# One GpSimd power in place of eleven VectorE operations for every inverse square root of a hybrid decoder layer

## The chip, the cores and the metric

The kernel runs on one core of a Trainium2 chip. The metric is the device time of one execution in microseconds (us). An engine's name in the profile is PE (TensorE, matrix products; PEld is its weight load), DVE (VectorE), ACT (ScalarE), POOL (GpSimd) and SP (SyncE, which here issues the DMAs). Each engine runs its own list of instructions in the order written down at build time; engines wait for each other only through semaphores.

## The reference, cut to what matters

One layer on x of shape (4096, 1024), float32:

```python
h    = rmsnorm(x, g_pre) * (1 + scale) + shift            # norm 1: one value per token
proj = h @ w_in                                            # one input projection, split among three mixers
attn = sliding_window_attention(...) * silu(ag)            # 8 query heads, window 128
y    = rwkv7(...)                                          # 4 heads of 64, delta-rule state
y    = (y - mean) * rsqrt(var + 64e-5) * ln_w + ln_b       # norm 2: one value per token and head
o    = gated_linear_attention(...)                         # 4 heads of 64
o    = o * rsqrt(mean(o * o) + 1e-5) * norm_w              # norm 3: one value per token and head
z    = concat(attn, rwkv, gla) @ w_out
out  = x + gate * rmsnorm(z, g_post)                       # norm 4: one value per token
```

The four `rsqrt` are what the change touches. (The keys of the RWKV mixer are normalised too, but through ScalarE's Ln and Exp, and stay as they are.)

## The kernel before, in words

The 4096 tokens are cut into 16 tiles of 256 (`NS` = 16, `NT` = 256). The program has two big parts.

In the first part (0 to about 1080 us) every tile passes through stages that are Python generators: `stage_a` (norm 1 of x, transposes, `hT`), `stage_p` (the input projections for the two linear mixers), `stage_d` (decays and gates), `stage_qa`, `stage_qb`, `stage_qc` (the RWKV chunk matrices and a triangular inverse, with two trips through DRAM), `stage_q2` (the RWKV state recurrence and norm 2), `stage_r` (gated linear attention and, in `gla_norm`, norm 3), `stage_v`, `stage_k`. Beside them `stage_c` splits the weights of the second part into two float16 halves and `stage_g` computes the adaLN gate on GpSimd. Tiles overlap: while one is in its recurrence, others are in their projections.

In the second part (about 1080 us to the end) each tile has `stage_s` (attention), `stage_m` (the gated mix, scaled and split into float16 halves) and `stage_p2` (gates, q, k, v of the next tiles and the output projection, `outp`). `outp` ends each half tile of 128 tokens with `norm` (norm 4, one column), and in the last tile with `last_norm`, whose result scales the last rows that are written out. For the first half in the last tile (`h` = 1) ScalarE scales and GpSimd adds x in two halves of 512 columns; for the other (`h` = 0) VectorE does both in one operation per half.

`rsqrt(y, v, n)` works on n columns of 128 partitions: n = 2 in `stage_a` (`msx` to `rsx`), 8 in `gla_norm` (`og` to `orr`) and in `stage_q2` (`ve` to `yr`), 1 in `norm` (`sy` to `ry`). It starts from the bit trick with the constant tile `magic` (a shift into tile `nwi`, a subtraction) and makes three Newton steps of three operations each through tile `nwt`: eleven VectorE instructions. `last_norm` has the same in nine (tiles `ln0` to `ln2`, `ln` in the profile), where the ninth also multiplies by `oi`. In all 78 calls of `rsqrt` (16 with n = 2, 32 with n = 8, 30 with n = 1) and two of `last_norm` are executed. A fallback for extreme gates, which calls the same helpers in a loop, is in the program but is not entered with these inputs.

The order on each engine is fixed by a planner, `Order`. `note` books every instruction with a cost (`occ`, how long it holds its engine; `lat`, until others may use the result); `pin`, called once for each part, simulates the five engines as a list scheduler: whichever engine is free takes, of its ready instructions, the one that comes first in the program (shifted by a lag for some stages), and the order that results is pinned. So a changed cost or a changed engine of one instruction changes the order of others too. GpSimd's costs before:

```python
        elif e == "Pool":
            if name == "memset":
                st.occ = 0.06
            elif name == "tensor_copy":
                st.occ = 0.25 if n <= 2 else 0.11 + 0.95e-3 * n
            else:
                st.occ = 0.42 + 1.5e-3 * n if n <= 512 else 1.85e-3 * n
            st.lat = st.occ + 0.05
```

GpSimd's other work in the first part: `tensor_tensor` for `ATm` (`stage_qb`, 32 partitions), `qb` (`stage_r`) and the gate (`gaw`, `gacc`), copies for `tf`, `TT`, `zs`, `zl`, `bl` (the last column of the tile before). In the second part it copies `kT` once a tile and adds x in `last_norm`.

Nearly all instructions are recorded through one helper, so they have line L334 in the profile; the tiles' names tell them apart.

Of the kernel before, what the change touches and what calls it, by code (L numbers as in the profile page):

```python
# [12 lines left out]
F32 = mybir.dt.float32  # L13
BF16 = mybir.dt.bfloat16
I32 = mybir.dt.int32
AF = mybir.ActivationFunctionType
ALU = mybir.AluOpType
# [4 lines left out]
P = 128  # L22
# [41 lines left out]
class Order:  # L64
# [34 lines left out]
    def note(self, eng, name, outs, ins, func, r):  # L99

        st = Step()
        st.ins, st.eng, st.table, st.array, st.bytes, st.then = r.ins, str(eng.engine).split(".")[-1], None, None, 0, []
        st.joint = self.joint
        st.half, st.rank = None, len(self.steps) + self.lag
        e, o = st.eng, outs[0]
        on_psum = [a for a in ins if str(a.tensor.space) == "PSUM"]
        n = max(math.prod(a.shape[1:]) for a in [o, *ins[:1]])
        cols = len([a for a in ins[1:] if math.prod(a.shape[1:]) == 1]) if n > 1 else 0
        if e == "PE":
            f32, lhs = ins[0].dtype == F32, self.region(ins[0])  # L110
            n = math.prod(o.shape[1:])
            _, p0, p1, _ = self.region(o)
            rows, cs = (lhs[1] // 32, (lhs[2] + 31) // 32), (p0 // 32, (p1 + 31) // 32)
            rows, cs = [(0, 4) if b - a > 2 else (a, b) for a, b in (rows, cs)]
            mode = (rows[1] - rows[0], cs[1] - cs[0])
            took = n * (2 if f32 else 1) / 2400 + 0.003
            took = max(took, 0.056 if not f32 else 0.0 if mode[1] < 4 else 0.109 if n > 16 else 0.21)
            issue = 0.017 if f32 and mode == (1, 2) else 0.009 if f32 and mode[0] == 1 else 0.007
            cells = [4 * a + b for a in range(*rows) for b in range(*cs)]
            st.array = (mode, cells, 2 if f32 and name == "matmul" else 1, took, issue)  # L120
            st.occ = st.lat = 0.0
        elif e == "SP":
            st.bytes = math.prod(ins[0].shape) * SIZE[ins[0].dtype]
            kb = st.bytes / 1024
            st.occ = 0.47
            st.lat = next((t for k, t in ((8, 1.9), (32, 2.0), (128, 2.3), (256, 2.6), (512, 3.5)) if kb <= k), 4.8)
        elif e == "Activation":
            st.occ = (0.05 if on_psum else 0.093) + 0.093 * (len(ins) - 1) + 0.832e-3 * n
            st.lat = st.occ + 0.1
            if len(outs) > 1:  # L130
                st.occ += 0.187
                st.lat = st.occ + 0.02
            st.table = LN_TABLE if func == AF.Ln else EXP_TABLE if func in (AF.Exp, AF.Tanh) else None
        elif e == "Pool":
            if name == "memset":
                st.occ = 0.06
            elif name == "tensor_copy":
                st.occ = 0.25 if n <= 2 else 0.11 + 0.95e-3 * n
            else:
                st.occ = 0.42 + 1.5e-3 * n if n <= 512 else 1.85e-3 * n  # L140
            st.lat = st.occ + 0.05
        else:
            if name == "tensor_reduce":
                n = math.prod(ins[0].shape[1:])
            fast = name in ("tensor_scalar", "tensor_single_scalar") and not on_psum and o.dtype == F32
            fixed, rate = 0.065 + 0.06 * (cols > 0), 1.04e-3
            if fast:
                rate = 0.53e-3
            elif name == "transpose":
                fixed = 0.09  # L150
            elif name == "memset":
                fixed, rate = 0.05, 0.3e-3
            elif name == "tensor_tensor" and len(o.shape) == 3 and o.shape[2] <= 16 and n > 16:
                fixed, rate = 0.09, 1.55e-3
            st.occ = fixed + rate * n
            st.lat = st.occ + 0.085

        k, st.needs, st.turn = len(self.steps), {}, []
        out_r, in_r = [self.region(a) for a in outs], [self.region(a) for a in ins]
        if e in ("Activation", "DVE"):  # L160

            st.half = (out_r[0][1], in_r[0][1] if e == "Activation" and in_r and out_r[0][2] - out_r[0][1] <= 64 else None)
        tiles = {a.tensor.name: a.tensor for a in [*outs, *ins]}

        if e == "SP" and self.behind is not None:
            st.turn.append(self.behind)

        def need(j, data=False):
            st.needs[j] = st.needs.get(j, False) or data

        for t, tensor in tiles.items():
            if t not in self.known:
                self.known.add(t)
                if t in self.held and tensor.tag:
                    held = self.slots.setdefault((tensor.owner_uid, tensor.tag), [])

                    if held and self.users.get(held[-1]):
                        st.turn.append(self.users[held[-1]][0])
                    if len(held) == self.held[t]:
                        for j in self.users.get(held.pop(0), ()):  # L180
                            need(j)
                    held.append(t)
            elif t in self.held and self.users.get(t):
                st.turn.append(self.users[t][0])
            if str(tensor.space) == "PSUM":
                for j in self.users.get(t, ()):
                    need(j)

        def meet(a, b):
            return a[1] < b[2] and b[1] < a[2] and (a[3] is None or a[3] & b[3])  # L190

        def covered(a, b):
            return b[1] <= a[1] and a[2] <= b[2] and (a[3] is None or not a[3] & ~b[3])

        for a in in_r:
            for w, j in self.wrote.get(a[0], ()):
                if meet(a, w):
                    need(j, True)
        for a in out_r:
            if a[3] is not None:  # L200
                for old in (self.wrote, self.read):
                    for w, j in old.get(a[0], ()):
                        if meet(a, w):
                            need(j)
                    old[a[0]] = [(w, j) for w, j in old.get(a[0], ()) if not covered(w, a)]
            self.wrote.setdefault(a[0], []).append((a, k))
        for a in in_r:
            self.read.setdefault(a[0], []).append((a, k))
        for t in tiles:
            self.users.setdefault(t, []).append(k)  # L210
        st.needs.pop(k, None)
        self.steps.append(st)
# [186 lines left out]
def hybrid_kernel(ctx, tc, x, rows, ada1, adaw, w1, wl, w2, wo, cst, abias, out):  # L399
    nc = tc.nc  # L400
    model = Model(tc)
    V = Lane(model, nc.vector, *LANES[0])
    S = Lane(model, nc.scalar, *LANES[1])
    G = Lane(model, nc.gpsimd, *LANES[2])
# [7 lines left out]
    cp = pool_of(ctx, "const", 1)  # L412
    dp = pool_of(ctx, "dram", 1, space=DRAM)
    st = pool_of(ctx, "small", 3)
# [7 lines left out]
        a, b = VC[name]  # L422
        return vt[:, a:b] if j is None else vt[:, a + j : a + j + 1]

    magic = cp.tile([P, 16], I32, name="magic")
    V.memset(magic, 0x5F3759DF)

    def rsqrt(y, v, n):
        ii = st.tile([P, 16], I32, tag="nwi", name="nwi")
        tt = st.tile([P, 16], F32, tag="nwt", name="nwt")  # L430
        V.tensor_single_scalar(ii[:, :n], v.bitcast(I32), 1, op=ALU.logical_shift_right)
        V.tensor_tensor(y.bitcast(I32), magic[:, :n], ii[:, :n], op=ALU.subtract)
        for _ in range(3):
            V.tensor_mul(tt[:, :n], y, y)
            V.scalar_tensor_tensor(tt[:, :n], tt[:, :n], -0.5, v, op0=ALU.mult, op1=ALU.mult)
            V.scalar_tensor_tensor(y, tt[:, :n], 1.5, y, op0=ALU.add, op1=ALU.mult)

    def pow2(sc, inv, ss):
        e = st.tile([P, 1], I32, tag="p2e", name="p2e")
# [1437 lines left out]

    def last_norm(f, h, sums, xt):

        v, y, t = [st.tile([P, 1], F32, tag=f"ln{n}", name=f"ln{n}") for n in range(3)]  # L1880
        V.scalar_tensor_tensor(v, sums[:, 0:1], 1e-6, sums[:, 1:2], op0=ALU.add, op1=ALU.add)
        V.tensor_single_scalar(t.bitcast(I32), v.bitcast(I32), 1, op=ALU.logical_shift_right)
        V.tensor_tensor(y.bitcast(I32), magic[:, 0:1], t.bitcast(I32), op=ALU.subtract)
        for c in (3.0, 12.0, 768.0):
            V.scalar_tensor_tensor(t, y, y, v, op0=ALU.mult, op1=ALU.mult)
            V.scalar_tensor_tensor(y, t, -c, y, op0=ALU.add, op1=ALU.mult)
        V.scalar_tensor_tensor(y, y, -1.0 / 8192, f["oi"], op0=ALU.mult, op1=ALU.mult)
        z, r0 = f["end"][h], (NS - 1) * NT + h * P
        for cols in (slice(0, 512), slice(512, 1024)):
            if h:  # L1890
# [176 lines left out]
    with tc.If(flag == 0):  # L2067
# [42 lines left out]
        with tc.For_i(0, NS, 1) as iv:  # L2110
# [9 lines left out]
            for j in range(2):  # L2120
                for n in (2 * j, 2 * j + 1):
                    z = fmx[j][:, 2 * (n % 2) : 2 * (n % 2) + 2, :].rearrange("p b n -> p (b n)")
                    V.scalar_tensor_tensor(z, z, g_h[n], F[0]["ag"][:, 2 * n : 2 * n + 2, :].rearrange("p b n -> p (b n)"),
                                           op0=ALU.mult, op1=ALU.mult)
                S.activation(fbk[:, 0, 0:4], fmx[j], AF.Square, accum_out=fss[:, j : j + 1])
            fsc, foi = mix_scale(fss)
            for j in range(2):
                S.activation(fbk[:, 0, 4 * j : 4 * j + 4], fmx[j], AF.Identity, scale=fsc)
                V.scalar_tensor_tensor(fbk[:, 1, 4 * j : 4 * j + 4], fmx[j], fsc, fbk[:, 0, 4 * j : 4 * j + 4],
                                       op0=ALU.mult, op1=ALU.subtract)  # L2130
# [110 lines left out]
```

## Time and profile before

| what | value |
|---|---|
| device time, median of 3 runs | 2062.37 us (2061.8 to 2066.6) |
| span of the profiled execution, first to last instruction | 2056.7 us; its device time is not listed apart |
| PE busy | 1950.2 us, 95% |
| DVE busy | 1590.3 us, 77% |
| ACT busy | 1130.8 us, 55% |
| POOL busy | 220.5 us, 11% |
| mean granted TensorE clock | 0.986 |

Busy time is a share of the span in which an engine executed something. An engine that is not the bound may idle at no cost. "Idle before, releaser" names what ended an engine's wait. Pipelined matmuls overlap, so a busy PE is not a PE at its peak.

### The profile page before, as it was taken

To read this page: it belongs to the slowest core of one execution; us is meant where nothing else is said; L and a number is where in the kernel's file an instruction comes from. 1 tells how busy PE (TensorE), PEld (TensorE's weight loads), DVE (VectorE), ACT (ScalarE), POOL (GpSimd) and SP (SyncE) were. 2 spreads that over 40 slices of the span, in tenths; PEclk is the share of its full clock that TensorE was granted. 3 is DMA by queue.
4 is the path that set the end of the run, shared out by engine and by line. 5 is a ranking of instruction groups with operands and counts; after the bars stand their busy time and mean duration, and the time that the engine had idled before them with its cause. 6 is when DMAs were issued, how large, how long until landed. Compare 5 with 4: busy or idle time off the path is not lost.

```text
span 2056.7 us, 61151 instructions
## 1 busy us (share of the span) xinstructions
PE 1950.2 (95%) x25123; PEld 1517.8 (74%) x25123; DVE 1590.3 (77%) x5120; ACT 1130.8 (55%) x2609; POOL 220.5 (11%) x405
## 2 busy tenths in 40 slices
PE   6899999999999999999898999999999999999997
PEld 3778787778787778887677677777787777777783
DVE  5877877787778986777667887887777877778877
ACT  5867666667767765664334544444444443444543
POOL 1511112321111121111100000000000000000000
PEclk9999999999999999999999999999999999999999
DMA  9433331433413332113433433433334343334314
GB/s 377 139 106 106 106 94 39 145 124 100 142 61 109 124 93 70 60 53 102 134 109 126 153 112 129 127 127 113 110 115 145 115 130 104 119 121 142 111 46 175
DMA packets 151714, 242.06 MB, mean 118 GB/s; under 512 B 48514, under 2 KB 100226, under 8 KB 147204
## 3 DMA queue, kind: packets, MB, share of 16 engines
q1 hardware_dynamic: 151284, 237.56, 35.6%
q8 instruction: 199, 3.26, 0.7%
q14 instruction: 87, 0.71, 0.1%
q10 hardware_dynamic: 144, 0.52, 0.1%
HBM read 177.20 MB, written 60.82 MB: 116 GB/s over the span
## 4 chain that ended last, share of the span: by engine, by line
PE 62%; DVE 21%; ACT 6%; DMA 6%; issue 3%; SPq 2%; DVEq 0%; POOL 0%; ACTq 0%; POOLq 0%
PE gp L334 16%; PE op L334 12%; PE zz L334 6%; PE qp L334 3%; PE lp L334 3%; PE pv L334 3%; PE kp L334 2%; PE gqk L334 2%; PE sc L334 2%; DVE mtp L334 2%; DVE q L334 2%; PE ovp L334 2%; DVE pr L334 2%; SPq L334 2%; DMA xt<-in_x 1%
## 5 line engine op out<-in xcount | busy, mean ns | idle before, releaser
L334 PEld LDWEIGHTS <-mtp 128*128 128x128 f16 x1344 | 130.4, 98 | 141.8 <-issue 4.6
L334 PE MATMUL op<-o,mtp 128*128 128x512 f16 x768 | 172.3, 379 | 0.1
L334 ACT ACTIVATE pr<-pr,nm,lsc 128x256 f32<-128x256 f32 (+1 forms) x256 | 149.2, 585 | 30.9 <-DVE nm L334 30.8
L334 PE MATMUL op<-ov,mtp 128*128 128x512 f16 x576 | 143.1, 379 | 1.3 <-DMA ov<-woscr 0.8
L334 PEld LDWEIGHTS <-hT 128*128 128x128 f16 x1536 | 118.9, 100 | 26.7 <-DVE kg L334 5.3
L334 DVE CUSTOM_DVE_ANT_0 pr<-sc,ab,kept 128x256 f32<-128x256 f32 (+1 forms) x256 | 108.5, 476 | 10.9 <-PE sc L334 10.2
L334 PE MATMUL pv<-gvh,hT 128*128 128x272 f16 x512 | 102.2, 291 | 6.4 <-DVE kg L334 4.5
L334 DVE TENSOR_TENSOR yv<-op,yv 128x512 f32<-128x512 f32 x105 | 70.4, 682 | 47.8 <-PE op L334 33.6
L334 ACT ACTIVATE ag<-gp,gh 128x512 f32<-128x512 f32 x64 | 43.7, 682 | 111.7 <-PE gp L334 111.7
L334 POOL COPY kT<-kT 128x512 f16<-128x512 f16 x15 | 10.2, 682 | 862.0 <-DVE kT L334 862.0
L334 PE MATMUL gqk<-hT,gqkh 128*128 128x256 f16 x512 | 90.3, 276 | 6.0 <-issue 4.2
L334 ACT ACTIVATE mtp<-yv,oi 128x1024 f16<-128x1024 f32 x30 | 34.3, 1144 | 111.8 <-DVE yv L334 111.3
L334 PE MATMUL qp<-hT,q1h 128*128 128x256 f16 x512 | 87.7, 276 | 5.9 <-DVE kT L334 5.9
L334 PE MATMUL lp<-hT,Lh 128*128 128x256 f16 x512 | 92.9, 276 | 0.2 <-ACT vg L334 0.2
L334 PE MATMUL zz<-hT,kh 128*128 128x256 f16 x512 | 92.3, 274 | 0.0
L334 PE MATMUL zz<-hT,vh 128*128 128x256 f16 x512 | 89.1, 275 | 3.4 <-DVE zb L334 3.4
L334 DVE SCALAR_TENSOR_TENSOR ag<-ag,gp 128x512 f32<-128x512 f32 x64 | 43.8, 684 | 62.4 <-ACT ag L334 62.3
L334 PE MATMUL zz<-hT,rh 128*128 128x256 f16 x512 | 91.8, 279 | 0.0
L334 PE MATMUL gp<-hT,q5h 128*128 128x256 f16 x512 | 87.6, 273 | 0.0
L334 PE MATMUL gp<-hT,q3h 128*128 128x256 f16 x512 | 85.5, 273 | 2.0 <-DVE yv L334 1.4
L334 PE MATMUL qp<-hT,q0h 128*128 128x256 f16 x512 | 85.2, 273 | 0.0
L334 PE MATMUL gp<-hT,q4h 128*128 128x256 f16 x512 | 84.9, 273 | 0.0
(460 smaller groups left out, 5981.7 us busy)
## 6 DMA issues: line engine op xcount, KB each, us to landing
ov<-woscr SPq DMA_DIRECT2D x96, 512.0 KB, 4.4
xt<-in_x SPq DMA_DIRECT2D x16, 1024.0 KB, 5.4
hscr<-hT SPq DMA_DIRECT2D x16, 1024.0 KB, 5.0
hT<-hscr SPq DMA_DIRECT2D x16, 1024.0 KB, 4.8
x<-in_x SPq DMA_DIRECT2D x30, 512.0 KB, 4.2
out<-yv SPq DMA_DIRECT2D x30, 512.0 KB, 2.9
cs<-in_w SPq DMA_DIRECT2D x56, 256.0 KB, 3.5
v<-vscr SPq DMA_DIRECT2D x128, 64.0 KB, 3.7
```

Of the source, the lines that this page charges most:

```text
L334: r = f(*args, **kw)
```

## The change

Each call of `rsqrt` becomes one GpSimd `tensor_tensor` with the operation `pow` and the exponent −0.5 from a constant tile. `last_norm` calls it too, and its ninth operation becomes a plain product with `oi`. The planner gets a cost for small GpSimd operations of at most 8 columns.

```diff
@@ Order.note, GpSimd's costs
             elif name == "tensor_copy":
                 st.occ = 0.25 if n <= 2 else 0.11 + 0.95e-3 * n
+            elif n <= 8:
+                st.occ = 0.33 + 0.165 * n
             else:
                 st.occ = 0.42 + 1.5e-3 * n if n <= 512 else 1.85e-3 * n
@@ hybrid_kernel
-    magic = cp.tile([P, 16], I32, name="magic")
-    V.memset(magic, 0x5F3759DF)
+    expo = cp.tile([P, 8], F32, name="expo")
+    V.memset(expo, -0.5)
 
     def rsqrt(y, v, n):
-        ii = st.tile([P, 16], I32, tag="nwi", name="nwi")
-        tt = st.tile([P, 16], F32, tag="nwt", name="nwt")
-        V.tensor_single_scalar(ii[:, :n], v.bitcast(I32), 1, op=ALU.logical_shift_right)
-        V.tensor_tensor(y.bitcast(I32), magic[:, :n], ii[:, :n], op=ALU.subtract)
-        for _ in range(3):
-            V.tensor_mul(tt[:, :n], y, y)
-            V.scalar_tensor_tensor(tt[:, :n], tt[:, :n], -0.5, v, op0=ALU.mult, op1=ALU.mult)
-            V.scalar_tensor_tensor(y, tt[:, :n], 1.5, y, op0=ALU.add, op1=ALU.mult)
+
+        G.tensor_tensor(y, v, expo[:, :n], op=ALU.pow)
@@ last_norm
-        v, y, t = [st.tile([P, 1], F32, tag=f"ln{n}", name=f"ln{n}") for n in range(3)]
+        v, y = [st.tile([P, 1], F32, tag=f"ln{n}", name=f"ln{n}") for n in range(2)]
         V.scalar_tensor_tensor(v, sums[:, 0:1], 1e-6, sums[:, 1:2], op0=ALU.add, op1=ALU.add)
-        V.tensor_single_scalar(t.bitcast(I32), v.bitcast(I32), 1, op=ALU.logical_shift_right)
-        V.tensor_tensor(y.bitcast(I32), magic[:, 0:1], t.bitcast(I32), op=ALU.subtract)
-        for c in (3.0, 12.0, 768.0):
-            V.scalar_tensor_tensor(t, y, y, v, op0=ALU.mult, op1=ALU.mult)
-            V.scalar_tensor_tensor(y, t, -c, y, op0=ALU.add, op1=ALU.mult)
-        V.scalar_tensor_tensor(y, y, -1.0 / 8192, f["oi"], op0=ALU.mult, op1=ALU.mult)
+        rsqrt(y, v, 1)
+        V.tensor_mul(y, y, f["oi"])
```

## The prediction

> **What bounds the kernel now.** I read the page first (shares, chain), then the span by stretches, then PE's waits, then the timeline of the tail.
>
> ```profile
> span 2056.7 us, 61151 instructions
> PE 1950.2 (95%) x25123; PEld 1517.8 (74%) x25123; DVE 1590.3 (77%) x5120; ACT 1130.8 (55%) x2609; POOL 220.5 (11%) x405
> ...
> PE 62%; DVE 21%; ACT 6%; DMA 6%; issue 3%; SPq 2%; DVEq 0%; POOL 0%; ACTq 0%; POOLq 0%
> ```
>
> PE is the bound and VectorE the second: a fifth of the chain that ended last runs through it. The busy times by stretch (length, then PE, PEld, DVE, ACT, POOL, each with its count) show where that matters.
>
> ```profile
> 120.00:600.00 480.00, 462.19 (x7365) 377.06 (x7364) 373.26 (x1359) 329.94 (x731) 96.31 (x183) 0.99 0.32 100
> 600.00:720.00 120.00, 112.15 (x1728) 90.77 (x1728) 107.99 (x376) 86.63 (x178) 19.74 (x38) 0.97 0.39 124
> 720.00:1080.00 360.00, 340.62 (x5571) 276.69 (x5570) 263.23 (x1010) 192.16 (x431) 53.70 (x105) 0.99 0.28 89
> ...
> 1202.00:1920.00 718.00, 707.43 (x7370) 541.59 (x7369) 560.89 (x1545) 319.28 (x804) 7.36 (x12) 1.00 0.37 120
> ```
>
> From 1202 to 1920 PE is busy 707.4 of 718 us (98.5%). From 120 to 1080 it is busy 462.19 + 112.15 + 340.62 = 915.0 of 960 us, so 45.0 us idle; VectorE is busy 373.26 + 107.99 + 263.23 = 744.5 us (77.6%), and 90% of the time between 600 and 720. No matmul goes, so those 45 us are the most that this stretch can give back. Who ends PE's waits (total us, times, longest us), first from 120 to 1080, then from 1202 to 1920:
>
> ```profile
> PE pv L334 <- DVE kg L334: 4.5, 3, 2.2
> ...
> PE op L334 <- DVE TT L334: 0.2, 1, 0.2
> ```
>
> ```profile
> PE sc L334 <- DVE m L334: 10.6, 12, 0.9
> ```
>
> In the first stretch 23 rows name VectorE as releaser; the first and the last stand above, and all sum to 30.0 us. In the second there is one row, a wait of 0.9 us once a tile for the scores' maxima.
>
> **What is removed.** 78 calls drop 11 VectorE instructions each, the two of `last_norm` eight each: 858 + 16 = 874 of 5120. Busy time by stretch of the nine per call that touch `nwt`, then of the two that touch `nwi`:
>
> ```profile
> 120.00:600.00 480.00, 33.03 (x207) 0.99 0.32 100
> 600.00:720.00 120.00, 8.24 (x54) 0.97 0.39 124
> 720.00:1080.00 360.00, 20.42 (x144) 0.99 0.28 89
> ...
> sum 2057.00, DVE 110.17; mean DVE 12.24
> ```
>
> ```profile
> 120.00:600.00 480.00, 7.38 (x46) 0.99 0.32 100
> 600.00:720.00 120.00, 1.96 (x12) 0.97 0.39 124
> 720.00:1080.00 360.00, 5.61 (x32) 0.99 0.28 89
> ...
> sum 2057.00, DVE 25.66; mean DVE 2.85
> ```
>
> That is 110.17 + 25.66 = 135.8 us of VectorE, 0.158 us an instruction, so 1.74 us a call. From 120 to 1080 it is 61.69 + 14.95 = 76.6 us.
>
> **What is added.** 80 GpSimd instructions: 32 with n = 1, 16 with n = 2, 32 with n = 8. No row shows a power. The nearest are GpSimd's products and sums, from 120 to 1080:
>
> ```profile
> L334 POOL TENSOR_TENSOR qb<-qg,kept 128x512 f32<-128x512 f32 x30 | 36.3, 1229 | 53.4 <-DVE qg L334 53.2
> ...
> L334 POOL TENSOR_TENSOR gacc<-gaw 128x128 f32<-128x128 f32 x8 | 4.8, 596 | 0.3
> ```
>
> The line through them, (1229 − 596)/384 = 1.65 ns a column, gives 0.40 us at n = 8: the lower end. The change itself books 0.50, 0.66 and 1.65 us for n = 1, 2, 8. Its entry for larger operations books 0.42 + 0.0015 x 512 = 1.19 us against the row's 1.229, so that table follows the chip, and I take its figures although no run here shows them; the upper end is twice that. A call with n = 8 then takes about as long as before, a call with n = 1 a third, and both leave VectorE free meanwhile. GpSimd's load in the stretch rises from 169.8 us (96.31 + 19.74 + 53.70) by some 60 to 230 of 960: it has room.
>
> **Term 1, 120 to 1080.** With 76.6 us less, VectorE's load falls to 667.9/960 = 69.6%. If lateness behind a loaded engine goes as load/(1 − load), it falls from 3.46 to 2.29, by 34%, and the 30.0 us of PE's waits by 10.2: one end (in plain proportion to the work it would be 3.1). Against it stand two new waits. VectorE's first use of the result now waits for GpSimd, with all that is queued behind it; and the power itself stands in GpSimd's queue among the copies `zs`, `zl`, `tf` and the products `ATm`, `qb`, so a power whose input is late holds those, and through `tf` and `bl` PE and VectorE. The planner sees both and puts other work in front; that cover is gone where a power is longer than booked. Second, the port. In the tail (VectorE's timeline, then ScalarE's and GpSimd's, then the chain):
>
> ```profile
> 2042.85 0.16 DVE L334 SCALAR_TENSOR_TENSOR ln<-lsum 128x1 f32<-128x1 f32 x1 [0.21 <-ACT pr L334]
> ...
> 2045.46 0.15 DVE L334 SCALAR_TENSOR_TENSOR ln<-lsum 128x1 f32<-128x1 f32 x1
> ...
> 2046.04 3.23 DVE L334 SCALAR_TENSOR_TENSOR ln<-ln,ln 128x1 f32<-128x1 f32 x6
> 2049.31 0.16 DVE L334 SCALAR_TENSOR_TENSOR ln<-ln,oi 128x1 f32<-128x1 f32 x1
> 2049.50 1.42 DVE L334 SCALAR_TENSOR_TENSOR pr<-pr,ln,xo 128x512 f32<-128x512 f32 x2
> ```
>
> ```profile
> 2045.97 1.33 ACT L334 ACTIVATE pr<-pr,ln 128x512 f32<-128x512 f32 x2 [0.57 <-DVE ln L334]
> ```
>
> ```profile
> 2046.77 2.49 POOL L334 TENSOR_TENSOR pr<-pr,xo 128x512 f32<-128x512 f32 x2 [139.79 <-ACT pr L334]
> ```
>
> ```profile
> 2046.75 0.17 DVE ln L334
> ...
> 2046.94 1.13 DVE ln L334
> ...
> 2048.09 1.20 DVE ln L334
> 2049.31 0.17 DVE ln L334
> ```
>
> Two VectorE operations on a single column take 1.13 and 1.20 us instead of 0.17, just while GpSimd's two additions of 1.25 us run. (The Trainium skill, "GPSIMD Engine Reference", section 8, Key points, has the reason: GpSimd shares its SBUF interfaces with VectorE, and VectorE instructions with two SBUF inputs contend. By that rule these rows agree, and each power, itself of two inputs, could hold up VectorE for its whole length.) Priced from the rows: the stretch has 90 instructions of the `nwi` rows, so 45 calls; 32 powers of 1.65 and 13 of 0.66 us are 61 us of possible stall, against 76.6 removed. But a power moves eight columns where those additions move 512, so I expect a third of it, 20 us. The net relief is 57 us: load 71.6%, lateness 2.52 instead of 3.46, minus 27% of 30.0: **−8 us**. With the whole stall the relief is 15 us and the gain about 2.5.
>
> The skill also speaks against the whole change: "GPSIMD Engine Reference", section 4.1, Engine selection, gives elementwise work to VectorE, GpSimd being about twice as slow. Instruction for instruction that fits a power of 1.65 us against one of 0.158; by it alone the change would lose, but it trades one for eleven.
>
> **Term 2, the tail.** After the last sums VectorE ends `v` at 2045.61 and begins the final scaling at 2049.50: 3.9 us, with nothing to hide them. A crossing between engines costs about 0.14 us (ScalarE's first half ends at 2045.97 + 0.66 = 2046.63, GpSimd starts at 2046.77). Power 0.50, two crossings 0.28, the product with `oi` 0.16 make 0.94: at best −2.9. But the other half's call is quicker too (`v` at 2042.85, so scaled from about 2043.9), its first addition holds GpSimd until about 2046.0, and the power comes behind it: −2.6. The second addition then runs beside the final scaling, of two SBUF inputs, and may hold it for up to a microsecond. I take **−2.3**; ends −2.9 and 0.
>
> **Term 3, the seams.** The last tile's norm 2 lies on the chain:
>
> ```profile
> 1070.72 0.18 DVE nwt L334
> ...
> 1072.33 0.18 DVE yr L334
> 1072.53 0.70 DVE ysb L334
> ```
>
> From 1070.1 to 1072.5 it is 2.4 us with two score operations between; with GpSimd 1.65 + 0.28 = 1.93, and the scores run meanwhile. **−1** (0 to −2). In the start-up VectorE is loaded and PE idles 8.3 of the 60 us from 60 to 120:
>
> ```profile
> 60.00:120.00 60.00, 51.72 (x531) 40.24 (x531) 46.17 (x126) 45.88 (x95) 27.73 (x39) 0.89 0.41 127
> ```
>
> One or two calls of norm 1 fall there: **−1** (0 to −2). The first tile's call, at 17 us, ends long before its weights are there: 0.
>
> **Term 4, 1202 to 1920.** Two calls a tile free some 3.5 us of VectorE, 78% loaded, but PE idles 10.6 us in the whole stretch, and its one wait is for the scores' maxima, with no norm in front. **0**; hidden behind PE. If the new order put a waiting product with `oi` ahead of the scores, every tile would pay.
>
> **The sum.** −8 − 2.3 − 1 − 1 = −12.3 us. The profiled span of 2056.7 becomes 2044.4; the median of the runs, 2062.4, is 5.7 us above that span, work outside first and last instruction that the change leaves alone. Forecast **2050 us**, 0.6% faster. A measurement here can tell about 0.3%, or 6.2 us, from no change.
>
> **Rivals.**
>
> *Hidden.* PE is 95% busy, and its records hide drains in small matmuls that no VectorE relief removes; or the port eats the relief. Then term 1 gives 2.5 at most, and with the tail the kernel comes to 2058, within 0.3%. For it: 15 us of the 45 idle are not VectorE's. Against: VectorE at 90% in 600 to 720, where PE lost 7.9 us.
>
> *VectorE was the true limit.* The chain's 21% and the stretch at 90% speak for it: the 30.0 us of waits go nearly wholly, as each late operation makes the next late. −25 − 4 gives 2033. Against: PE's other 15 us, and the second part, which cannot follow.
>
> *The power is slow.* At 3.3 us for n = 8 and 1.3 for n = 2, 32 x 3.3 + 13 x 1.3 = 122 us of waiting on VectorE in the stretch against 76.6 removed: its load rises to 790/960 = 82%, lateness from 3.46 to 4.6, a third more: +10; the tail still gains 1.5. 2071, slower. It decides from where a call costs VectorE more than 76.6/45 = 1.7 us of standing still. For it: no row shows a power, and the port rows. Against: the booked figure, and a planner that fills the wait.
>
> *The order shifts.* All costs and one engine change, so every list is written anew. In the second part one tile's order repeats (its wait stands 12 times in the row): 0.8 us of PE's wait more a tile (a wait like the one of 0.9 us today) would be +10 and give about 2061 after the gains; 0.8 us less, 2040. For it: the pattern repeats; against: PE's idle time is 1.5% there.
>
> **How the numbers follow.** The forecast case (2038 to 2056) has 0.48; VectorE as the limit, 0.12; hidden, 0.24, within 0.3%; the order against us, 0.06; the slow power, 0.10. Faster 0.60, same 0.25, slower 0.15, the order's case lying on both sides of the line. The range must leave out no more than 0.2: 2034 to 2068 reaches over most of the limit's case, all of the hidden one and the milder end of the slow one; the forecast's own range is 2038 to 2056.
>
> **What would show it.** Right: VectorE's busy time near 1460 us with some 875 instructions fewer, GpSimd's near 290; PE idle from 120 to 1080 down from 45 to about 37; the start of the final scaling about 1.5 us after the last `v`; the tile's period from 1202 on unchanged. Wrong: powers well over 1.65 us; VectorE's products with `oi` or the scalings of `xt`, `osb`, `ysb` with idle time ended by POOL; two-input VectorE operations stretched beside a power; copies `zs` and `tf` late; the first part as long as before although VectorE is lighter; a longer period in the second.

## The result, and the profile after

The changed kernel takes 2051.81 us (median) against 2060.22 us for the kernel before on the same chip: ratio 0.9960, 95% interval 0.9948 to 0.9972, so 8 us or 0.4% faster. The forecast was 2050. One of its ten executions took 6744 us; its cause is not known, and it is in neither the ratio nor any comparison below (the median without it is 2051.5). The profiled execution took 2052.67 us, with a span 6.0 us shorter than before.

The page, its span, engines and chain:

```profile
span 2050.7 us, 60367 instructions
...
PE 1952.7 (95%) x25123; PEld 1515.4 (74%) x25123; DVE 1485.5 (72%) x4246; ACT 1128.2 (55%) x2609; POOL 306.3 (15%) x485
...
PE 58%; DVE 17%; ACT 8%; issue 3%; DMA 2%; SPq 1%; POOL 1%; DVEq 0%; ACTq 0%; POOLq 0%
```

VectorE has 874 instructions fewer, as counted beforehand, and is 104.9 us less busy; GpSimd has 80 more and 85.8 us more. The matmuls are the same 25123. The span by stretches (length, PE, PEld, DVE, ACT, POOL, each with its count), of the kernel after:

```profile
120.00:600.00 480.00, 463.51 (x7438) 375.32 (x7436) 350.62 (x1130) 332.96 (x742) 127.72 (x208) 0.99 0.34 105
600.00:720.00 120.00, 112.69 (x1707) 92.24 (x1705) 100.03 (x295) 85.85 (x176) 32.05 (x45) 0.99 0.37 114
720.00:1080.00 360.00, 342.33 (x5530) 277.21 (x5528) 243.48 (x829) 194.59 (x442) 72.18 (x117) 0.99 0.28 92
...
1202.00:1920.00 718.00, 707.16 (x7267) 538.21 (x7266) 523.57 (x1301) 322.90 (x818) 19.27 (x34) 1.00 0.37 120
```

In the stretch that the prediction looked at, PE gains only 3.6 us (918.5 against 915.0), while VectorE falls from 744.5 to 694.1 us. To find the other microseconds, the same view in three coarser stretches, first of before, then of after (the last three numbers of a row are the granted clock, the DMA engines' share and GB/s):

```profile
0.00:120.00 120.00, 92.50 (x772) 63.20 (x773) 83.76 (x279) 84.16 (x165) 38.62 (x64) 0.90 0.66 234
120.00:1080.00 960.00, 914.97 (x14658) 744.52 (x14657) 744.49 (x2743) 608.73 (x1338) 169.75 (x325) 0.99 0.32 99
1080.00:1202.00 122.00, 113.44 (x1166) 83.83 (x1164) 97.25 (x271) 59.07 (x155) 2.26 (x2) 0.97 0.42 139
```

```profile
0.00:120.00 120.00, 92.96 (x792) 63.30 (x793) 80.42 (x251) 83.70 (x165) 42.56 (x67) 0.91 0.66 234
120.00:1080.00 960.00, 918.52 (x14670) 744.77 (x14667) 694.13 (x2251) 613.40 (x1357) 231.95 (x370) 0.99 0.32 101
1080.00:1202.00 122.00, 118.69 (x1279) 88.31 (x1280) 98.06 (x237) 55.96 (x144) 5.39 (x6) 0.99 0.40 128
```

By 1202 us PE has done 9.3 us more work: 0.5 in the start-up, 3.6 in the middle, 5.2 at the seam between the two parts. Three marks in the traces say where it stays. The matmuls for `kp` (the keys of a coming tile) from which the tiles follow each other every 62.5 us, in both kernels, begin at 1211.4 before and at 1202.6 after (−8.8). The last `kp` comes at 1938.8 and 1930.1 (−8.7). But from there to PE's last end it is 105.0 us before and 109.5 after: the last tile gives 4.5 us back. From PE's last end to the end of VectorE's last instruction it is 7.16 and 5.94 us (−1.2). Together: −5.4 of the span's −6.0 us; the rest lies behind that instruction.

What the powers cost, by tile `expo` (ns: least, median, most; first and last start), and who waited for GpSimd behind them:

```profile
L336 POOL TENSOR_TENSOR ry<-sy,expo x30: 539/544/1519, 1138.6 to 2019.5; 128x1 f32<-128x1 f32 x30
L336 POOL TENSOR_TENSOR rsx<-msx,expo x16: 695/698/839, 17.3 to 825.3; 128x2 f32<-128x2 f32 x16
L336 POOL TENSOR_TENSOR orr<-og,expo x16: 1632/1638/2160, 125.3 to 1020.4; 128x8 f32<-128x8 f32 x16
L336 POOL TENSOR_TENSOR yr<-ve,expo x16: 1631/2008/2308, 185.2 to 1064.2; 128x8 f32<-128x8 f32 x16
...
  DVE ry L336: 9.0, 14
  DVE xt L336: 7.1, 10
  DVE ln L336: 2.4, 2
  DVE ysb L336: 2.1, 2
```

The booked 0.50, 0.66 and 1.65 us were 0.54, 0.70 and 1.64, except that `yr` takes 2.01. VectorE waits for a power 28 times, 20.6 us in the whole run.

### The profile page after: what moved, and what is told of

Its sections match the earlier page's. It is cut to its first block, busy times and chain, and to the rows that moved or that the text cites. A ratio compares the mean times of both kernels' runs of the same rounds, so it can differ in the third digit from the quotient of the medians.

```text
span 2050.7 us, 60367 instructions
## 1 busy us (share of the span) xinstructions
PE 1952.7 (95%) x25123; PEld 1515.4 (74%) x25123; DVE 1485.5 (72%) x4246; ACT 1128.2 (55%) x2609; POOL 306.3 (15%) x485
## 4 chain that ended last, share of the span: by engine, by line
PE 58%; DVE 17%; ACT 8%; issue 3%; DMA 2%; SPq 1%; POOL 1%; DVEq 0%; ACTq 0%; POOLq 0%
PE gp L336 16%; PE op L336 12%; PE zz L336 5%; PE qp L336 4%; PE lp L336 2%; PE gqk L336 2%; PE pv L336 2%; PE sc L336 2%; PE kp L336 2%; DVE mtp L336 2%; DVE q L336 2%; PE ovp L336 2%; DVE pr L336 2%; SPq L336 1%; PE atp L336 1%
## 5 line engine op out<-in xcount | busy, mean ns | idle before, releaser
L336 ACT ACTIVATE mtp<-yv,oi 128x1024 f16<-128x1024 f32 x30 | 34.5, 1149 | 154.1 <-DVE yv L336 113.4
L336 POOL TENSOR_TENSOR ry<-sy,expo 128x1 f32<-128x1 f32 x30 | 18.7, 623 | 588.2 <-DVE sy L336 588.2
L336 PE MATMUL gp<-hT,q6h 128*128 128x256 f16 x512 | 85.2, 273 | 0.0
```

The costliest lines, as they stand in the source:

```text
L336: r = f(*args, **kw)
```

## Where in the kernel: one part alone

Three theories stood at first: the gain comes from VectorE's relief in the first part (A), from the tail and the seams (B), or from the rewritten order alone (C). Each run below was timed in five rounds, beside the kernel before.

**The power in the first part only** (norm 4 and `last_norm` keep their VectorE operations):

```diff
+    def newton(y, v, n):      # the eleven VectorE operations
...
-        rsqrt(ry, sy, 1)
+        newton(ry, sy, 1)
```

> The power only in the first part (norms 1, 2, 3: 48 calls); norm 4 and the last norm keep the VectorE steps. Theory A (VectorE's queue in the first part is what the change relieves, PE limits the rest): nearly all of the gain, -6 to -9 us against before, the second part starting 7 to 8 us earlier and its period unchanged. Rival B (the gain is in the tail and the seams): 0 to -2 us. Rival C (it comes from the rewritten order, not from the relief): any number within some 6 us of before, and no link with VectorE's load.

Measured: 2049.52 against 2057.45 us, ratio 0.9961 (0.9947 to 0.9976). All of the gain is there. This speaks against B but not against C, since the first part here has the order of the kernel after. For the same reason it shows how far a single profiled execution can be trusted: with one and the same first part, PE is busy 920.7 us in the middle stretch here and 918.5 in the kernel after, and the tiles' regular `kp` begin at 1205.1 and 1202.6. The next run shares its first part with before in the same way and has 915.6 against 915.0, and 1207.6 against 1211.4. So the 8.8 us found above is between 2.5 and 8.8 by the choice of the two executions.

**The power in norm 4 and `last_norm` only:**

```diff
-        rsqrt(orr, og, 8)
+        newton(orr, og, 8)
-            rsqrt(rsx, msx, 2)
+            newton(rsx, msx, 2)
-            rsqrt(yr, ve, 8)
+            newton(yr, ve, 8)
```

> The power only in norm 4 and the last norm (32 calls); the first part keeps the VectorE steps. Theory A: 0 to -2 us, the tail's -1.2 and some at the start of the second part, with the last tile able to eat it. Rival B: -5 to -8 us. Rival C: anything within some 6 us.

Measured: 2058.11 us, ratio 1.0004 (0.9995 to 1.0014): no gain. Inside, two things offset each other. In this kernel the last tile takes 109.3 us where the first-part kernel takes 105.1, and the tail 5.94 us instead of 7.15. Much of what happens in the last tile is in SP's queue. SP's DMA issues in the first-part kernel, with nothing of norm 4 on GpSimd:

```profile
2016.13 8.01 SPq L336 DMA_DIRECT2D ov<-woscr  x4
2024.19 0.42 SPq L336 DMA_DIRECT2D out<-yv  x1
2024.66 0.42 SPq L336 DMA_DIRECT2D x<-in_x  x1
2027.39 0.32 SPq L336 DMA_DIRECT2D ov<-woscr  x1
```

The same queue in the kernel after, and PE:

```profile
2015.49 1.61 SPq L336 DMA_DIRECT2D ov<-woscr  x2
2020.69 0.34 SPq L336 DMA_DIRECT2D out<-yv  x1
2021.08 0.42 SPq L336 DMA_DIRECT2D x<-in_x  x1
2021.60 1.88 SPq L336 DMA_DIRECT2D ov<-woscr  x2
```

```profile
2022.97 2.10 PE L336 MATMUL op<-o,mtp 128*128 128x512 f16 x9
2027.57 2.74 PE L336 MATMUL op<-ov,mtp 128*128 128x512 f16 x6 [2.50 <-DMA ov<-woscr]
```

With a norm that is ready sooner, the planner puts the write of its rows (`out<-yv`) and the load of the next `x` ahead of two loads of `ov`, the output weights. The norm's last addition ends at 2020.66, SP stands behind it, the two `ov` loads go out at 2021.60, and PE waits 2.50 us for them (0.8 before, 0.9 in the first-part kernel). The six matmuls after the wait take 2.74 us instead of the 1.46 of the same six elsewhere, because the granted clock (the third number from the end) is 0.54 just then:

```profile
2027.50:2031.00 3.50, 3.43 (x9) 1.29 (x10) 0.70 (x1) 0.00 (x0) 0.00 (x0) 0.54 0.46 183
2031.00:2034.00 3.00, 3.00 (x16) 1.37 (x14) 0.69 (x1) 0.00 (x0) 0.00 (x0) 1.00 0.60 198
```

The longer last tile goes with norm 4's power in every kernel run here: in the six with VectorE's norm 4 (before, its three other orders, the first-part kernel, the one without Newton steps) it is 104.7 to 105.1 us; in the eight with the power it is 107.5 to 109.8. Such a slow stretch follows the wait in only three of these eight, the three with 109.3 to 109.8 us. The kernel after at 0.060 (below) waits 2.47 us as well and keeps a clock of 1.00; what decides it was not tried. Against before's 105.0 us, norm 4's power costs 2.5 to 4.8 us in the last tile, and it saves 1.2 in the tail. In the kernel after, the longer wait for `ov` is 1.7 of the 4.5 us and the slow matmuls 1.6; the rest is small waits and matmuls elsewhere in the tile.

## How much is relief, and how much is the wait for GpSimd

**Newton steps left out** (before, with two VectorE operations a call and no power):

```diff
-        for _ in range(3):
-            V.tensor_mul(tt[:, :n], y, y)
-            V.scalar_tensor_tensor(tt[:, :n], tt[:, :n], -0.5, v, op0=ALU.mult, op1=ALU.mult)
-            V.scalar_tensor_tensor(y, tt[:, :n], 1.5, y, op0=ALU.add, op1=ALU.mult)
```

> Before with the Newton steps left out: two VectorE operations a call (shift and subtraction) and no GpSimd power, so the inverse roots are the rough first guess, some 3% off. It has almost the whole relief of VectorE and none of GpSimd's latency. Theory A with a small price of the power: within 3 us of the changed kernel, -6 to -11 us against before. If GpSimd's latency and VectorE's standing still eat half of the relief (the share that the prediction set aside): -12 to -18 us. Rival C: no relation to the relief.

Measured: 2036.85 us, ratio 0.9898 (0.9879 to 0.9916), 21 us faster, more than either forecast with a number had allowed (−6 to −11 and −12 to −18). With no power in it the short norm is worth more than twice the change, although VectorE is less relieved (710.89 us in the middle stretch against 694.13):

```profile
120.00:1080.00 960.00, 922.12 (x14779) 749.65 (x14778) 710.89 (x2351) 611.55 (x1360) 166.59 (x326) 0.99 0.32 102
```

This run also limits what the late loads explain. Its norm 4 is short too, SP sends `out<-yv` (2007.81) and `x` ahead of two `ov` loads (2008.71), and PE waits 2.1 us for `ov` in its last tile; yet that tile takes 105.0 us, as before. So late loads need not lengthen the last tile.

**Every power with eight columns done twice:**

```diff
+        if n == 8:
+            twice = st.tile([P, 8], F32, tag="twice", name="twice")
+            G.tensor_tensor(twice, v, expo[:, :n], op=ALU.pow)
         G.tensor_tensor(y, v, expo[:, :n], op=ALU.pow)
```

> The changed kernel with every power of eight columns done twice on GpSimd, the first into a tile that nobody reads: 32 x 1.65 = 53 us more of GpSimd and every result 1.65 us later, booked by the planner. Theory A (the wait is covered by other work): within 3 us of the changed kernel, so -5 to -9 us against before. If GpSimd's latency is on the path: +0.13 us of PE for each us of standing still at the least, and up to 1.65 us a call, +7 to +50 us against the changed kernel.

Measured: 2041.16 us, ratio 0.9919 (0.9905 to 0.9933): doubled, it is faster than the change itself. GpSimd is busy 293 us in the middle stretch, VectorE waits 11.6 us for `yr` instead of 2.1, and the kernel gains 17 us instead of 8. None of the theories of cost explains a gain by more work; the planner books the second power too and writes another order. That made the order the suspect.

**Not booked** (the planner's entry for small GpSimd operations left out; eight columns are then booked at 0.43 us):

```diff
-            elif n <= 8:
-                st.occ = 0.33 + 0.165 * n
```

> The changed kernel without the planner's new entry, so that a power of eight columns is booked 0.43 instead of 1.65 us and VectorE's first use of the result is put too early. Theory D (the booked length makes the planner put other work in front, and that cover is worth what the powers would cost): VectorE stands still about 1.2 us in each of 32 calls, 0.13 us of PE for each at least, so 5 us or more worse than the changed kernel, -3 us or worse against before. Theory C: no link with the booking, -16 to 0 us.

Measured: 2082.27 against 2057.98 us, ratio 1.0123 (1.0106 to 1.0140): 25 us slower than before, with the same instructions as the change. VectorE's groups with their idle time, then PE's waits from 120 to 1080 us, then the stretch:

```profile
L334 DVE TENSOR_TENSOR ysb<-ysb,yr 128x512 f32<-128x512 f32 x16 | 11.1, 696 | 19.2 <-POOL yr L334 17.8 <-POOL vg L334 1.4
L334 DVE TENSOR_TENSOR osb<-osb,orr 128x512 f32<-128x512 f32 x16 | 11.1, 695 | 15.8 <-POOL orr L334 15.8
```

```profile
PE yt L334 <- DVE ysb L334: 12.2, 10, 1.6
PE Xp L334 <- DVE D L334: 8.5, 4, 5.4
PE ot L334 <- DVE osb L334: 8.0, 8, 1.6
```

```profile
120.00:1080.00 960.00, 894.72 (x14341) 722.13 (x14338) 686.08 (x2197) 602.27 (x1322) 234.31 (x369) 0.99 0.30 95
```

VectorE's product follows right behind its power, stands 17.8 + 15.8 = 33.6 us, and PE loses 918.5 − 894.7 = 23.8 us in the stretch against the change. In the booked order those two waits were 2.1 us together. So the cover that the planner finds for the powers is worth some 33 us (2082.3 against 0.9960 times 2058.0), four times what the change gains and three times what another order alone gave (below).

**Booked at twice the cost** (3.3 us for eight columns, done once):

```diff
-                st.occ = 0.33 + 0.165 * n
+                st.occ = 0.33 + 0.165 * n if n < 8 else 3.3
```

> The changed kernel with a power of eight columns booked 3.3 us (as two) but done once. Theory D (a longer booking gives more cover; that is what made the doubled powers faster): as fast as the doubled powers or faster, -14 to -20 us against before. Theory C (the doubled powers met a lucky order): anywhere from 0 to -17 us, no link with the booking. Theory A alone: -8 +-3 us.

Measured: 2045.74 us, ratio 0.9946 (0.9931 to 0.9960), so −11 us. The wait for `yr` falls to 1.1 us from 2.1, but the −14 to −20 us that theory D asked for are not there: a longer booking than the true one buys little. The 3 us more than the change are no more than another order gives, as the next runs show.

## How much is the order

The planner's fixed cost of a VectorE operation was changed, and nothing else; the instructions are the same, in another order.

```diff
-            fixed, rate = 0.065 + 0.06 * (cols > 0), 1.04e-3
+            fixed, rate = 0.07 + 0.06 * (cols > 0), 1.04e-3
```

Before and after with 0.070:

> Before, with one planner constant changed: a VectorE operation's fixed cost booked 0.070 instead of 0.065 us. No instruction is added or taken away; only the order differs. Theory A (the relief of VectorE's queue sets the gain): within 3 us of before. Theory C (a rewritten order by itself moves the first part by several us, so the gain of 8 and the 16 of the doubled powers hold a share of luck): up to 8 us either way.

> The changed kernel with the same planner constant, 0.070 instead of 0.065 us: same instructions, another order. Theory A: -8 +-3 us against before, as the changed kernel. Theory C: anywhere from 0 to -17 us.

Before and after with 0.060 and with 0.075:

> Before's instructions, only the planner's fixed VectorE cost at 0.060 instead of 0.065, so another order of the same work. So far: 0.065 before 0, after -8 us; 0.070 before -10, after -12. Theory A (relief carries the gain, the order only adds a scatter smaller than it): this stands within 5 us of before, and e10_after_060 is 4 to 10 us faster than this one. Theory C (order luck carries it): this lies anywhere from -12 to +8, and the difference to e10_after_060 may have either sign.

> The change with the planner's fixed VectorE cost at 0.060. Theory A: 4 to 10 us below e9_before_060, near -8 to before. Theory C: within -12 to +8 of before, on either side of e9_before_060.

> Before's instructions with the planner's fixed VectorE cost at 0.075. Theory A: like 0.070, about -8 to -10 to before, since a slightly larger booked cost fits the VectorE durations better; e12_after_075 again lower by 2 to 8. Theory C: anywhere from -12 to +8, unrelated to the value at 0.070.

> The change with the planner's fixed VectorE cost at 0.075. Theory A: 2 to 8 us below e11_before_075, about -12 to before. Theory C: either side of e11_before_075. With the pairs at 0.060, 0.065 and 0.070 four differences after minus before are there: theory A wants all four below zero with a mean of -4 to -8, theory C a mean within 3 us of zero.

Measured, as a ratio to before with its interval, the same in us (times 2058), the profiled span, and PE's busy time in two stretches:

| order | kernel | ratio to before | us | span | PE 120 to 1080 | PE 0 to 1202 |
|---|---|---|---|---|---|---|
| 0.060 | before's | 0.9967 (0.9956 to 0.9979) | −6.8 | 2051.5 | 916.57 | 1128.33 |
| 0.060 | after's | 0.9952 (0.9937 to 0.9966) | −9.9 | 2045.0 | 921.71 | 1132.46 |
| 0.065 | before | 1 | 0 | 2056.7 | 914.97 | 1120.91 |
| 0.065 | after | 0.9960 (0.9948 to 0.9972) | −8.2 | 2050.7 | 918.52 | 1130.17 |
| 0.070 | before's | 0.9952 (0.9936 to 0.9968) | −9.9 | 2048.8 | 915.82 | 1125.96 |
| 0.070 | after's | 0.9945 (0.9932 to 0.9958) | −11.3 | 2041.7 | 923.08 | 1136.13 |
| 0.075 | before's | 0.9964 (0.9951 to 0.9976) | −7.4 | 2051.4 | 915.43 | 1123.55 |
| 0.075 | after's | 0.9917 (0.9901 to 0.9932) | −17.1 | 2037.6 | 921.37 | 1135.26 |

The four differences of the pairs are −3.1, −8.2, −1.4 and −9.7 us: all one way, with a mean of −5.6 us and a standard deviation of 4.0, so ±4 us on the mean by two standard errors of four; a strict 95% interval for so few is ±6.3 and just reaches zero. The relief theory asked for all four below zero and a mean of −4 to −8; luck alone asked for a mean within 3 us of zero. The mean speaks for relief. But much of what that theory said of single runs fell: before at 0.070 and 0.060 should have stood within 3 and 5 us of before (−9.9 and −6.8), after at 0.070 at −5 to −11 (−11.3), the pair at 0.075 at 2 to 8 us apart (9.7), and of the pair at 0.060 only the medians (5.3 us) and not the ratios (3.1) reach the 4 us it asked for. All three other orders of before are 7 to 10 us faster than before: its order was an unlucky one, and a new order of the old instructions gains as much as the change did. PE's busy time in the middle stretch scatters less: before's four lie within 1.6 us, and the change adds 5.1, 3.6, 7.3 and 5.9, on average 5.5 us (±2.5 by the strict interval). The rows of the pair at 0.070, before's order and after's:

```profile
120.00:1080.00 960.00, 915.82 (x14690) 745.33 (x14687) 746.33 (x2752) 614.03 (x1358) 168.07 (x325) 0.99 0.32 101
```

```profile
120.00:1080.00 960.00, 923.08 (x14775) 747.21 (x14769) 704.43 (x2263) 614.68 (x1362) 234.05 (x371) 0.99 0.32 102
```

So of the 8 us about five or six are the change's on the average of four orders, shown for PE's work in the first part and likely for the time; where a single pair lies is the order's.

One more rival is in the runs' clocks. Executions of one kernel differ in their mean granted clock, and the time goes with it: of before's executions in the last round the fastest had 2054.3 us at 0.988 and the slowest 2062.3 at 0.984, and over all runs here it is about 1 us for each 0.001. In the pair at 0.060 the mean clocks are 0.9867 and 0.9893. Brought to one clock by that figure (an estimate, since a kernel that waits less may also be granted more), the means of the pairs at 0.060, 0.070 and 0.075 differ by −1.7, −2.5 and −10.3 us: the sign stays, but the first two hardly tell.

The kernel after at 0.075 is the fastest with the whole computation, level with the doubled powers: 2040.47 us, 0.8% below before and, by the ratios, 0.4% below after. The first-part power in that order was not tried.

## Why the prediction was right, and where it was not

The time (2050, measured 2051.8), the sign and the main reason hold: VectorE is lighter, PE waits for it less in the first part, and the second part's period does not move. That the time came so near is in part luck. The forecast was a gain of 12.3 us on a median of 2062.4; the kernel before took 2060.2 beside the change, and the gain was 8.4. The terms missed in both directions, and the order, which was not in the sum, moves either kernel by as much as the whole gain.

**Term 1 (−8 in the middle stretch)** measured −3.6 here and −5.5 over four orders. Two of its steps were wrong and nearly cancelled. The 135.8 us of small operations were 104.9 us of VectorE's busy time, 0.120 us each and not 0.158: neighbours in the queue overlap at their ends, and a view of the small ones alone counts that overlap as theirs. And the 20 us of stalls at the port were not there. VectorE around the power of `yr` at 362.87 us, then GpSimd:

```profile
362.62 0.17 DVE L336 TENSOR_SCALAR ve<-mv 128x8 f32<-128x8 f32 x1
362.70 0.68 DVE L336 TENSOR_TENSOR ysb<-ysb,mv 128x512 f32<-128x512 f32 x1
363.30 0.23 DVE L336 TENSOR_REDUCE TT<-tsc 128x8 f32<-128x80 f32 x1
363.45 0.74 DVE L336 SCALAR_TENSOR_TENSOR ch<-cs,wsc,ch 128x512 f16<-128x512 f32 x1
```

```profile
362.87 2.01 POOL L336 TENSOR_TENSOR yr<-ve,expo 128x8 f32<-128x8 f32 x1 [1.64 <-DVE ve L336]
```

The subtraction with two SBUF inputs, `ysb<-ysb,mv`, takes 0.68 us, as without a power beside it. Over the run 306 VectorE instructions overlap a power and have others of their kind that do not; against the medians of those they take 0.3 us less in all. (The Trainium skill, "GPSIMD Engine Reference", section 8, Key points, has GpSimd contend with such VectorE instructions. The trace agrees that they meet, but here it is the power that pays: 2.01 us instead of 1.64.) The relief was thus 744.5 − 694.1 = 50.4 us against the 57 taken. The step from relief to time was too steep as well: load 72.3%, so lateness 2.61 for 3.46, should cut the 30.0 us of PE's waits on VectorE by a quarter; the 17 rows after, of which the first and the last stand here, sum to 24.9, a cut of 17%:

```profile
PE gqk L336 <- DVE zb L336: 4.5, 2, 2.3
...
PE op L336 <- DVE Gst L336: 0.2, 1, 0.2
```

**Term 3 (−1 and −1 at the seams)** was too small: −0.5 in the start-up and −5.2 from 1080 to 1202. It priced one chain of norm 2, and not that the seam depends on the order: before's four orders have PE busy 113.4 to 119.6 us there (after's 118.7 to 120.8), so this is the piece with most of the luck in it.

**Term 2 (−2.3 in the tail)** measured −1.2. The steps named are there, in another order. GpSimd, then VectorE, in the tail of the kernel after:

```profile
2038.96 0.54 POOL L336 TENSOR_TENSOR ln<-ln,expo 128x1 f32<-128x1 f32 x1 [17.90 <-DVE ln L336]
2040.53 2.91 POOL L336 TENSOR_TENSOR pr<-pr,xo 128x512 f32<-128x512 f32 x2 [1.03 <-ACT pr L336]
2043.40 0.54 POOL L336 TENSOR_TENSOR ln<-ln,expo 128x1 f32<-128x1 f32 x1
```

```profile
2041.80 0.43 DVE L336 SCALAR_TENSOR_TENSOR ln<-lsum 128x1 f32<-128x1 f32 x1 [0.70 <-ACTq L2059]
2043.98 0.16 DVE L336 TENSOR_TENSOR ln<-ln,oi 128x1 f32<-128x1 f32 x1 [1.74 <-POOL ln L336]
2044.17 1.41 DVE L336 SCALAR_TENSOR_TENSOR pr<-pr,ln,xo 128x512 f32<-128x512 f32 x2
```

The last `v` ends at 2042.23 and the scaling starts at 2044.17: 1.94 us instead of the 1.5 predicted and the 3.9 before. The prediction let the power in behind the first addition; it came behind both, and VectorE waited 1.74 us. Also `v` itself waits 0.70 us and takes 0.43 instead of 0.16 beside the additions.

**Term 4 (0 from 1202 to 1920)** was right, but the sum had no term for the last tile, and there the change lost 4.5 us. The prediction named neither SP's queue nor the `ov` loads, nor what the clock does after a wait. This is the step that was missing, not mis-sized: a norm that ends sooner moves its DMA write forward in SP's order. In the kernel after, the longer wait and the slow matmuls behind it are 3.3 of the 4.5 us.

**The rivals.** "Hidden" (2058) fell in its time and in its port, but it was right that most of PE's 45 us of idle time in the middle stretch stay: 41.5 do. "The power is slow" was a true mechanism with the wrong price: the powers are nearly as fast as booked, but the run without the booking shows what that rival feared, VectorE standing still, 25 us on the other side. "The order shifts" had 0.06 and was priced in the second part alone; the order by itself moved before by 7 to 10 us, as much as the gain that was measured. "VectorE was the true limit" is not settled: the run without Newton steps came to 2037, near that rival's 2033, though with less relief of VectorE than the change. And one power against one VectorE operation, 1.65 against 0.158 us, is ten to one: the prediction's remark that this fits a factor of two was wrong.

**What stays open** is how the 21 us of that run divide between the shorter chains, the missing powers and a lucky order: it was made in one order only. What makes the seam so sensitive, why the longer last tile does not come with the late loads alone, and what lowers the clock behind some of the waits were not tried either.

## What to carry to other kernels

Moving a chain of small operations to an idle engine pays only if something covers its latency there: here 50 us less on VectorE brought PE five or six on average, while 34 us of uncovered waits cost it 24. When a planner writes the order, run each version under a few neighbouring cost constants before believing a difference of half a percent; one pair in one order could have shown 1 us or 10. And follow a result that becomes ready sooner to the DMA that it triggers, and see what that DMA is queued ahead of.

## What the runs showed of the hardware

A GpSimd power on 128 partitions took 0.54, 0.70 and 1.64 us for 1, 2 and 8 columns. It stretched beside some longer VectorE operations that were already running: 15 of the 16 `yr` powers, which overlap the subtraction `ysb<-ysb,mv`, took 1.94 to 2.31 us, and the one that ran after the subtraction took 1.63. VectorE operations that began while a power was running kept their time, those with two SBUF inputs too, such as `ch<-cs,wsc,ch` above with 0.74 us (0.75 on average). The worst case is on one column, GpSimd and then VectorE in the kernel after:

```profile
2016.51 0.54 POOL L336 TENSOR_TENSOR ry<-sy,expo 128x1 f32<-128x1 f32 x1 [82.59 <-DVE sy L336]
2019.55 1.52 POOL L336 TENSOR_TENSOR ry<-sy,expo 128x1 f32<-128x1 f32 x1 [2.49 <-DVE sy L336]
```

```profile
2019.43 1.23 DVE L336 TENSOR_TENSOR yv<-yv,x 128x1024 f32<-128x1024 f32 x1
2021.10 0.16 DVE L336 TENSOR_TENSOR ry<-ry,oi 128x1 f32<-128x1 f32 x1 [0.44 <-POOL ry L336]
```

The same power takes 0.54 us alone and 1.52 us beside a long addition that began just before it. In the tail of the kernel before it was the other way round: VectorE's single column took 1.13 us beside GpSimd's addition. In these rows the small operation that comes second waits for the large one; why was not tried. And after PE had waited 2.50 us, its clock was 0.54 for the next 3.5 us in the kernel after, but 1.00 after a wait of 2.47 us in the kernel after at 0.060.
